# Gates and branch projections with tokens stationary instead of weights

## The chip, the core and the metric

The kernel runs on one core of a Trainium2 chip. Its engines run side by side, each through a queue of its own: PE (TensorE, the matmuls; PEld are its weight loads), DVE (VectorE), ACT (ScalarE), POOL (GpSimd), and SP, which here only issues DMAs. The metric is device microseconds of one execution, the median of several. Before the change it is 1636.45 us (three runs, 1636.2 to 1637.2).

## What is computed

Two layers of an encoder on 256 tokens of 1024 channels, all in f32. A layer has a mixer, a cross-attention into 256 memory tokens, and a SwiGLU feed-forward part. The change is in the mixer:

```python
h = rmsnorm(x)
q, k, v, z, xbc, dt, f_in, gate_logit = split(h @ w_in)
y_attn    = attention(q, k, v) @ w_b_attn             # inner width 512
y_ssd     = gated_norm(ssd(xbc, dt), z) @ w_b_ssd     # inner width 2048
y_fourier = re_fft2(f_in) @ w_b_fourier               # inner width 1536
gates     = sigmoid(gate_logit + gate_bias)           # (256, 3, 1024)
merged    = gates[:, 0] * y_attn + gates[:, 1] * y_ssd + gates[:, 2] * y_fourier
x         = x + merged @ w_out
```

## The kernel before

**Numbers.** Each f32 matrix is split in two parts of the type that the array takes at full speed, hi (rounded) and lo (the rest). A product is three matmuls: hi*hi, hi*lo, lo*hi.

**The weight stream.** All weights lie in HBM in the order of use, in pieces of up to [128, 2048] f32 (1 MB). `load_next` (L312) issues a piece's DMA on SP, `split_next` makes hi with ACT (L322) and lo with DVE (L323); three raw and three split pieces are held. ORDER gives the mixer's order: Fourier columns, B/C, k0, x0, gate 2 (G2), Fourier branch (BF), the columns of q, k, v, x and z mixed, gate 0 (G0) before z0, z2, z3, then the attention branch (BA), gate 1 (G1), and last the SSD branch.

**Two loops of matmuls.** `lin` (L352 to L354) keeps 128 tokens stationary and moves 512 weight columns; the result is rows of tokens. It goes through a piece for the first half of the tokens and then for the second, so two of the four accumulation banks (acc) fill at a time. `lina` (L413 to L415) keeps a [128, 128] block of weights stationary and moves the 256 tokens; the result has the channels on the partitions, which is the layout (F) that the next product needs. Before the change gates and branches are done with `lina`: ACT's tanh takes gate logits out of PSUM with the bias as a per-partition operand (L1013), DVE multiplies the branch's result with 1 + tanh and adds it to the merged sum (L1028 to L1031), and behind the SSD branch ACT and DVE make hi and lo of the sum (L1113, L1114).

**Background tasks.** Convolution, SSD, attention, Fourier and norms are Python generators in four lanes. When the program is built, `pump` is called twice a piece and puts out steps of them for a credit in microseconds; a step that is about to put TensorE's work on fresh results first skips some calls (LATER, SOON), and a step that needs SBUF slots waits until enough are free. `drain_until` and `drain` put out what is left by force: before BF, before BA (all of attention: logits L602, transposes of the softmax L637, values L647, transposes of the joined output L667, hi and lo of it L487 and L488), and before the SSD branch everything (SSD matmuls L847 and L848, results L850 to L852, product with silu(z) L869, squares L870, power L445, scaling L876, transposes L885, hi and lo L487 and L488). Then the framework orders each engine's instructions; an engine runs its own in that order.

Of the kernel before, what the change touches and what calls it, by code (L numbers as in the profile page):

```python
# [43 lines left out]
# ---------------------------------------------------------------- weight stream  # L44
# A piece is [128, nk * n]: nk k-tiles x n columns, at most 2048.
# [3 lines left out]
def stream_plan():  # L49
# [17 lines left out]
    def blocks(w, kt, n):  # L67
        for n0 in range(0, 1024, n):
            plan.append((w, 0, kt, n0, n))

    for tok in ORDER:
# [3 lines left out]
        elif k == "G":  # L75
            for c in range(4):
                wide("w_in", G0 + 1024 * g + 256 * c)
        elif tok == "BF":
            blocks("w_branch_fourier", 12, 128)
        elif tok == "BA":  # L80
            blocks("w_branch_attn", 4, 512)
# [10 lines left out]
    blocks("w_branch_ssd", 16, 128)  # L92
# [20 lines left out]
POFF = [sum(PSIZE[:i]) for i in range(NPIECE + 1)]  # L113


def pack_weights(inputs):
    out = np.empty((L, POFF[-1]), np.float32)
    for l in range(L):
        for i, (w, k0, nk, n0, n) in enumerate(PLAN):
            a = np.asarray(inputs[w])[l, k0 * P:(k0 + nk) * P, n0:n0 + n]  # L120
            out[l, POFF[i]:POFF[i + 1]].reshape(P, nk, n)[...] = a.reshape(nk, P, n).transpose(1, 0, 2)
    return out


# ---------------------------------------------------------------- constants of the shapes
# [8 lines left out]
def shape_consts():  # L134
# [6 lines left out]
    # distances between tokens of the halves by parity: rows for the offsets -1, 0, 1  # L141
    # entry i + j of a row belongs to query i and key 127 - j
# [26 lines left out]
# ---------------------------------------------------------------- kernel  # L169
@with_exitstack  # L170
def trunk(ctx: ExitStack, tc: tile.TileContext, a, out):
# [16 lines left out]
    # Slots of 4 KB and 2 KB for all that comes and goes; a slot's tiles follow in the order of emission.  # L188
# [43 lines left out]
    # ---- background tasks, fed between weight pieces: lanes of generators, each lane in its own order.  # L232
    # A task yields the vector time of what it put out, or LATER or SOON before work of TensorE on what is still under way,
    # or the numbers of 4 KB and 2 KB slots that it is about to take.
# [10 lines left out]
    def step(only=None, force=True):  # L245
        """One step of a background task; False if there is none to run."""
# [48 lines left out]
    # ---- weight stream  # L295
# [4 lines left out]
    def parts(i, n):  # L300
        """The first pieces come by k-tiles, so that the products can start early."""
# [45 lines left out]
    def ordered():  # L347
        """Several accumulations in one bank: TensorE keeps their order."""
        return tc.manual_schedule(engines={mybir.EngineType.PE})
# [6 lines left out]
    # activations in F layout: lists of (hi, lo) tiles [128, 4, 256] per four k-tiles  # L356
    def lin(act, npieces, on_done, nk=8, seg=None, us=BUDGET, par=False, before=None, mid=None):
        """act(kt) -> (hi, lo, index). Pieces come from the stream; on_done(tt, chunk, psum)."""
# [37 lines left out]
    def lina(act, npieces, on_done, us=BUDGET):  # L396
        """Weights stationary: [columns, tokens]. A piece has all k-tiles; on_done(first column, psum [128, nb, 256])."""
# [26 lines left out]
    # ---- constants  # L424
# [12 lines left out]
    def bcast(src, n, tag=None, bufs=2):  # L437
        """A DRAM row of n values on all partitions."""
# [8 lines left out]
    # ---- RMS norm of [128, 1024] rows, then F layout  # L447
    sums = {}

    def square(tt, c):  # L450
        """Sum of the squares of half of X's columns."""
# [25 lines left out]
    def norms(n):  # L477
        """Goes on until no more than n norms are left."""
        drain_until(lambda: len(lanes["n"]) <= n, "n")

    def put_f(pt, hl, tt, scale=None, n=4, par=False):
        """psum [128, n*128] -> hi/lo of an F tile, token half tt."""
# [14 lines left out]
    # ======================================================================= start  # L497
# [40 lines left out]
    # ======================================================================= attention  # L538
    def attn_group(l, g, qt, kt_, vt, gqk, R):
        """qt, kt_, vt: [128, 2, 512] T layout. R: the groups joined so far."""  # L540
# [870 lines left out]
```

## Time and profile before

| | |
|---|---|
| median of the runs | 1636.45 us |
| span of the profiled execution | 1634.2 us |
| TensorE busy | 1618.7 us, 99% |
| VectorE busy | 1155.0 us, 71% |
| ScalarE busy | 972.1 us, 59% |
| GpSimd busy | 46.1 us, 3% |
| read from HBM | 294.44 MB, 181 GB/s |

Of the profiled execution only the span is told, from its first instruction to its last; its whole time is not, and the median stands 2.2 us over that span. A matmul's "us" is its way through a pipe that several share, so the distance of two starts tells what one costs. A wait is named by what ended it.

### The profile page before, as it was taken

The page shows a single profiled execution, that of the slowest core. Times are in us where ns is not written, and L with a number is a line of the kernel's source. Part 1 is how long each engine was busy: PE and PEld are TensorE (multiplying, and loading weights), DVE is VectorE, ACT ScalarE, POOL GpSimd, SP SyncE. Part 2 cuts the span into 40 slices and gives each one's busy share as a digit, 9 for nine tenths or more (in the row PEclk, how much of TensorE's full clock was granted, in tenths as well). Part 3 has the DMA queues.
Part 4 walks back from the last instruction along what each step waited for, and adds up shares of the span by engine and source line. Part 5 has one row for each costly group of instructions (what it writes and reads, how often), then busy time and mean ns, then how long its engine had stood idle before and what let it go on. Part 6 is the DMA issues. An engine that isn't in the chain of part 4 may idle for free.

```text
span 1634.2 us, 25737 instructions
## 1 busy us (share of the span) xinstructions
PE 1618.7 (99%) x10426; PEld 1464.2 (90%) x10426; DVE 1155.0 (71%) x1795; ACT 972.1 (59%) x1661; POOL 46.1 (3%) x47
## 2 busy tenths in 40 slices
PE   7999999999999999999999999999999999999998
PEld 6999988898998888999889999888989988889997
DVE  5898878787967665555477988778888676665543
ACT  6566667777745665444355667677786457554441
POOL 0000000000100100000000000000001001000000
PEclk9999999999999999999999999999999999999999
DMA  8445764545556544655553466645455555445552
GB/s 292 138 156 195 234 205 149 200 166 186 183 180 229 182 155 155 224 182 181 180 187 119 161 206 217 209 161 183 173 181 198 178 208 175 146 158 181 183 189 92
DMA packets 84878, 297.31 MB, mean 182 GB/s; under 512 B 7593, under 2 KB 46889, under 8 KB 54552
## 3 DMA queue, kind: packets, MB, share of 16 engines
q1 hardware_dynamic: 84760, 295.68, 52.9%
q8 instruction: 81, 1.33, 0.3%
q14 instruction: 37, 0.30, 0.1%
HBM read 294.44 MB, written 1.22 MB: 181 GB/s over the span
## 4 chain that ended last, share of the span: by engine, by line
PE 96%; ACT 2%; DVE 1%; DMA 0%; POOL 0%; issue 0%; SPq 0%; DVEq 0%; POOLq 0%
PE acc L354 15%; PE acc L352 15%; PE acc L353 15%; PE acc L414 13%; PE acc L413 13%; PE acc L415 13%; PE tp L847 2%; PE tp L352 1%; PE tp L354 1%; PE tp L353 1%; PE tp L848 1%; PE tp L472 1%; PE tp L647 1%; PE tp L602 1%; ACT wh L322 1%; ACT s L561 1%
## 5 line engine op out<-in xcount | busy, mean ns | idle before, releaser
L323 DVE TENSOR_TENSOR wl<-wr,wh 128x2048 fp32r<-128x2048 f32 (+2 forms) x260 | 573.5, 2208 | 295.3 <-ACT wh L322 294.1
L322 ACT CAST wh<-wr 128x2048 fp32r<-128x2048 f32 (+2 forms) x260 | 477.6, 1840 | 419.3 <-issue 186.5
L413 PE MATMUL acc<-s,wh 128*128 128x256 f32 x1856 | 527.8, 285 | 0.0
L414 PE MATMUL acc<-s,wh 128*128 128x256 f32 x1856 | 526.7, 284 | 0.0
L415 PE MATMUL acc<-s,wl 128*128 128x256 f32 x1856 | 525.6, 283 | 0.0
L352 PE MATMUL acc<-wh,s 128*128 128x512 f32 x1072 | 427.3, 399 | 0.0
L353 PE MATMUL acc<-wl,s 128*128 128x512 f32 x1072 | 423.8, 396 | 0.0
L354 PE MATMUL acc<-wh,s 128*128 128x512 f32 x1072 | 423.4, 395 | 0.0
L413 PEld LDWEIGHTS acc<-s,wh 128*128 128x128 f32 x1856 | 355.9, 192 | 1.6 <-issue 0.9
L414 PEld LDWEIGHTS acc<-s,wh 128*128 128x128 f32 x1856 | 356.1, 192 | 1.3 <-issue 0.5
L415 PEld LDWEIGHTS acc<-s,wl 128*128 128x128 f32 x1856 | 355.9, 192 | 0.0
L354 PEld LDWEIGHTS acc<-wh,s 128*128 128x128 f32 x1072 | 203.5, 190 | 41.5 <-issue 1.4
L352 PEld LDWEIGHTS acc<-wh,s 128*128 128x128 f32 x1072 | 203.8, 190 | 40.8 <-issue 1.9
L353 PEld LDWEIGHTS acc<-wl,s 128*128 128x128 f32 x1072 | 203.6, 190 | 40.5 <-issue 0.9
L688 DVE SCALAR_TENSOR_TENSOR s<-s,cw,s 128x254 f32<-128x254 f32 (+2 forms) x288 | 121.7, 476 | 1.1 <-ACT s L685 0.7
L819 ACT ACTIVATE s<-s,nacs 128x128 f32<-128x128 f32 x128 | 44.6, 393 | 12.3 <-DMA s<-dd 10.6
L352 PE MATMUL tp<-s,s 128*128 128x256 f32 (+1 forms) x176 | 50.3, 287 | 0.0
L354 PE MATMUL tp<-s,s 128*128 128x256 f32 (+1 forms) x176 | 49.9, 285 | 0.0
L353 PE MATMUL tp<-s,s 128*128 128x256 f32 (+1 forms) x176 | 49.7, 283 | 0.0
L822 ACT ACTIVATE s<-s,dt 128x128 f32<-128x128 f32 x128 | 43.9, 395 | 2.7 <-DVE s L603 2.1
L820 DVE SCALAR_TENSOR_TENSOR s<-s,nacs,s 128x128 f32<-128x128 f32 x128 | 41.5, 344 | 3.6 <-ACT s L819 3.6
L823 DVE SCALAR_TENSOR_TENSOR s<-s,dt,s 128x128 f32<-128x128 f32 x128 | 40.1, 344 | 0.0
(216 smaller groups left out, 1417.6 us busy)
## 6 DMA issues: line engine op xcount, KB each, us to landing
wr<-in_wstream SPq DMA_DIRECT2D x236, 1024.0 KB, 4.9
s<-dd SPq DMA_DIRECT2D x32, 512.0 KB, 4.4
wr<-in_wstream SPq DMA_DIRECT2D x16, 768.0 KB, 4.4
s<-vd SPq DMA_DIRECT2D x12, 256.0 KB, 5.7
wr<-in_wstream SPq DMA_DIRECT2D x8, 256.0 KB, 5.1
s<-in_ssd_norm_g SPq DMA_DIRECT2D x8, 256.0 KB, 5.3
s<-in_memT SPq DMA_DIRECT2D x4, 512.0 KB, 5.8
s<-in_c_dft SPq DMA_DIRECT2D x6, 256.0 KB, 5.0
```

Source lines behind the costliest of these rows:

```text
L322: A.copy(hi[:, c], raw[:, c])
L323: V.tensor_sub(lo[:, c], raw[:, c], hi[:, c].bitcast(F32))
L352: T.matmul(o, sh, mh, start=start, stop=False)
L353: T.matmul(o, sh, ml, start=False, stop=False)
L354: T.matmul(o, sl, mh, start=False, stop=stop)
L413: T.matmul(o, hi[:, w0:w0 + P], sh[:, k, :], start=kt == 0, stop=False)
L414: T.matmul(o, hi[:, w0:w0 + P], sl[:, k, :], start=False, stop=False)
L415: T.matmul(o, lo[:, w0:w0 + P], sh[:, k, :], start=False, stop=kt == npk - 1)
L688: V.scalar_tensor_tensor(v[:, b, i0:i1], u[:, b, i0 + k - 3:i1 + k - 3], c[:, k:k + 1], v[:, b, i0:i1], op0=ALU.mult, op1=ALU.add)
L819: A.activation(E[:, j, :], b[:, 1, :], AF.Identity, bias=nacs[:, tt, 32 + hf:33 + hf])
L820: V.scalar_tensor_tensor(E[:, j, :], b[:, 0, :], nacs[:, tt, hf:hf + 1], E[:, j, :], op0=ALU.add, op1=ALU.min)
L822: A.activation(W[:, j, :], cbd[:, tt, 0, :], AF.Copy, scale=dt[:, tt, hf:hf + 1])
```

## The change

Gates and the three branches go through `lin`. Their weights are packed in half pieces of four k-tiles by 512 columns (six pieces of 1 MB for the Fourier branch in place of eight of 768 KB). The bias rows are packed behind the weights; a gate loads its row on all partitions into a 4 KB slot, DVE adds it to the logits, and ACT's tanh follows in place. The merge is done in rows of tokens. Behind the SSD branch each [128, 512] part of the sum becomes a background task: four transposes on TensorE, then hi and lo (`put_f`). Two of the four must be out before the output projection begins, the others after its first piece.

```diff
-    def blocks(w, kt, n):
-        for n0 in range(0, 1024, n):
-            plan.append((w, 0, kt, n0, n))
+    def chunks(w, nh):
+        for n0 in (0, 512):
+            for h in range(nh):
+                half(w, n0, h)
     for tok in ORDER:
         k, g = tok[0], int(tok[1]) if len(tok) > 1 and tok[1].isdigit() else 0
         if k == "f":
             full("w_in", F0 + 512 * g)
         elif k == "G":
-            for c in range(4):
-                wide("w_in", G0 + 1024 * g + 256 * c)
+            full("w_in", G0 + 1024 * g)
+            full("w_in", G0 + 1024 * g + 512)
         elif tok == "BF":
-            blocks("w_branch_fourier", 12, 128)
+            chunks("w_branch_fourier", 3)
         elif tok == "BA":
-            blocks("w_branch_attn", 4, 512)
+            chunks("w_branch_attn", 1)
...
-    blocks("w_branch_ssd", 16, 128)
+    chunks("w_branch_ssd", 4)
...
+NBIAS = 3 * D
...
-    out = np.empty((L, POFF[-1]), np.float32)
+    out = np.empty((L, POFF[-1] + NBIAS), np.float32)
+    out[:, POFF[-1]:] = np.asarray(inputs["gate_bias"])
...
-        gbc = sm([P, 24], "gbc", bufs=1)
-        nc.sync.dma_start(gbc, a["gateb"][l])
-        V.tensor_scalar(gbc, gbc, 0.5, None, op0=ALU.mult)
...
         def gates(b):
-            ga = [s4([P, 4, S]) for _ in range(2)]
-            def f(n0, ps):
-                c = (n0 - G0) // P
-                for j in range(2):
-                    k = c + j - 8 * b
-                    A.activation(ga[k // 4][:, k % 4, :], ps[:, j, :], AF.Tanh, scale=0.5, bias=gbc[:, c + j:c + j + 1])
-            lina(hb, 4, f)
+            ga = [s4([P, D]) for _ in range(2)]
+            o = POFF[-1] + D * b
+            gbb = bcast(a["wstream"][l:l + 1, o:o + D], D)
+            c0 = (G0 + D * b) // 512
+            def f(tt, ch, ps):
+                cs = slice((ch - c0) * 512, (ch - c0) * 512 + 512)
+                g_ = ga[tt][:, cs]
+                V.tensor_add(g_, ps, gbb[:, cs])
+                A.activation(g_, g_, AF.Tanh, scale=0.5)
+            lin(hb, 4, f)
+            free(gbb)
             return ga
         mg = []
-        def branch(act, np_, ga, fin=None):
+        def branch(act, nh, ga, fin=None):
             first = not mg
             if first:
-                mg.extend(s4([P, 4, S]) for _ in range(2))
-            def f(n0, ps):
-                c, n = n0 // P, ps.shape[1]
-                g_, m_ = (t[c // 4][:, c % 4:c % 4 + n, :] for t in (ga, mg))
+                mg.extend(s4([P, D]) for _ in range(2))
+            def f(tt, ch, ps):
+                cs = slice(ch * 512, ch * 512 + 512)
+                g_, m_ = ga[tt][:, cs], mg[tt][:, cs]
                 if first:
                     V.scalar_tensor_tensor(m_, g_, 1.0, ps, op0=ALU.add, op1=ALU.mult)
                 else:
                     V.scalar_tensor_tensor(g_, g_, 1.0, ps, op0=ALU.add, op1=ALU.mult)
                     V.tensor_add(m_, m_, g_)
                 if fin:
-                    fin(c, n, m_)
-            lina(act, np_, f)
+                    fin(tt, ch, m_)
+            lin(act, 2 * nh, f, nk=4 * nh)
...
-                branch(fl(FT), 8, ga)
+                branch(fl(FT), 3, ga)
...
-                branch(fl(R["oT"]), 2, ga)
+                branch(fl(R["oT"]), 1, ga)
...
-        def merge_fin(c, n, m_):
-            hi, lo = (t[:, c % 4:c % 4 + n, :] for t in mT[c // 4])
-            A.activation(hi, m_, AF.Copy, scale=0.5)
-            V.scalar_tensor_tensor(lo, m_, 0.5, hi.bitcast(F32), op0=ALU.mult, op1=ALU.subtract)
-        branch(fl(yT), 8, ga, merge_fin)
-        free(*yT.values(), ga, mg)
+        merged = []
+        def merge_task(tt, ch, m_):
+            yield SOON
+            pt = tp()
+            for k in range(4):
+                T.transpose(pt[:, k * P:(k + 1) * P], m_[:, k * P:(k + 1) * P], idn)
+            put_f(pt, mT[ch], tt, scale=0.5)
+            merged.append((tt, ch))
+            yield 0.6
+        branch(fl(yT), 4, ga, lambda tt, ch, m_: bg(merge_task(tt, ch, m_)))
+        free(*yT.values(), ga)
+        def all_merged():
+            drain_until(lambda: len(merged) == 4, "s")
+            free(mg)
+        drain_until(lambda: len(merged) >= 2, "s")
...
-        lin(fl(mT), 4, residual(gbx, hx), seg=[1, 3])
+        lin(fl(mT), 4, residual(gbx, hx), seg=[1, 3], before=all_merged)
```

Three places in the order of the instructions. Numbers behind a name tell one buffer from another; `wh` and `wl` are parts of weights, `tp` the banks of the background tasks, `idn` the identity of a transpose.

TensorE before, at the last logits matmul (L602) of layer 0, and at the first matmul of its attention branch (L413), 61 wide matmuls later. At the logits:

```order
L354 MATMUL acc1_116<-wh403_4105,s4_9_137 128x512
L352 MATMUL acc1_116<-wh403_4105,s4_8_136 128x512
L353 MATMUL acc1_116<-wl404_4106,s4_8_136 128x512
L602 MATMUL tp1_112<-s4_409_4149,s2_415_4218 128x128
L354 MATMUL acc1_116<-wh403_4105,s4_9_137 128x512
L352 MATMUL acc2_117<-wh403_4105,s4_8_136 128x512
L353 MATMUL acc2_117<-wl404_4106,s4_8_136 128x512
```

At the branch, behind the z columns (acc0) and an SSD matmul (L848):

```order
L353 MATMUL acc0_115<-wl421_4301,s4_8_136 128x512
L354 MATMUL acc0_115<-wh420_4300,s4_9_137 128x512
L352 MATMUL acc0_115<-wh420_4300,s4_8_136 128x512
L353 MATMUL acc0_115<-wl421_4301,s4_8_136 128x512
L848 MATMUL tp1_112<-s2_438_4452,s4_173_1590 128x512
L354 MATMUL acc0_115<-wh420_4300,s4_9_137 128x512
L413 MATMUL acc1_116<-s4_430_4380,wh427_4372 128x256
L414 MATMUL acc1_116<-s4_431_4381,wh427_4372 128x256
```

Attention's later sets (L637, L647, L667) stand among the 61 and are not shown.

TensorE now, at the same logits matmul (L606), 11 wide matmuls before the z columns end:

```order
L358 MATMUL acc3_118<-wh415_3901,s4_9_137 128x512
L356 MATMUL acc0_115<-wh415_3901,s4_8_136 128x512
L606 MATMUL tp1_112<-s4_400_3696,s2_409_3818 128x128
L357 MATMUL acc0_115<-wl416_3902,s4_8_136 128x512
L358 MATMUL acc0_115<-wh415_3901,s4_9_137 128x512
L356 MATMUL acc0_115<-wh415_3901,s4_8_136 128x512
```

and from that end to the branch (L356 on acc1):

```order
L357 MATMUL acc0_115<-wl416_3902,s4_8_136 128x512
L358 MATMUL acc0_115<-wh415_3901,s4_9_137 128x512
L671 MATMUL tp0_111<-idn_121,s4_257_2347 128x128 x4
L641 MATMUL tp2_113<-idn_121,s2_410_3819 128x128 x4
L651 MATMUL tp3_114<-s4_322_2939,s2_411_3820 128x128 x4
L671 MATMUL tp1_112<-idn_121,s4_257_2347 128x128 x4
L852 MATMUL tp3_114<-s2_440_4126,s4_173_1481 128x512
L356 MATMUL acc1_116<-wh418_3933,s4_432_4044 128x512
L357 MATMUL acc1_116<-wl419_3934,s4_432_4044 128x512
```

The softmax's transposes (L641), the values (L651) and the joined output's transposes (L671) of the second half stand in one row between the last z column and the branch, with one SSD matmul (L852); before, they stood among z columns.

VectorE before, in that place, between the softmax's sums (L625) and the joining (L656, L657):

```order
L625 TENSOR_TENSOR rsum272_2695<-rsum272_2695,asc418_4237 128x4
L869 TENSOR_TENSOR s4_331_3275<-s4_331_3275,s4_419_4275 128x512
L626 TENSOR_TENSOR asc418_4237<-asc418_4237 128x4
L627 TENSOR_TENSOR rsum272_2695<-rsum272_2695,asc418_4237 128x4
L629 RECIPROCAL asc418_4237<-rsum272_2695 128x4
L630 TENSOR_TENSOR asc418_4237<-asc418_4237 128x4
L631 TENSOR_TENSOR asc418_4237<-asc418_4237 128x4
L656 TENSOR_SCALAR s4_270_2693<-s4_270_2693,asc418_4237 128x128 x4
L657 SCALAR_TENSOR_TENSOR s4_270_2693<-tp3_114,asc418_4237,s4_270_2693 128x128 x4
```

and now, between the sums (L629) and the joining (L660):

```order
L629 TENSOR_TENSOR rsum259_2349<-rsum259_2349,asc413_3838 128x4
L327 TENSOR_TENSOR wl426_3997<-wr417_3905,wh425_3996 128x2048
L630 TENSOR_TENSOR asc413_3838<-asc413_3838 128x4
L824 SCALAR_TENSOR_TENSOR s4_430_4006<-s4_428_4002,nacs112_941,s4_430_4006 128x128
L631 TENSOR_TENSOR rsum259_2349<-rsum259_2349,asc413_3838 128x4
L824 SCALAR_TENSOR_TENSOR s4_430_4006<-s4_428_4002,nacs112_941,s4_430_4006 128x128
L633 RECIPROCAL asc413_3838<-rsum259_2349 128x4
L824 SCALAR_TENSOR_TENSOR s4_430_4006<-s4_428_4002,nacs112_941,s4_430_4006 128x128
L634 TENSOR_TENSOR asc413_3838<-asc413_3838 128x4
L635 TENSOR_TENSOR asc413_3838<-asc413_3838 128x4
L824 SCALAR_TENSOR_TENSOR s4_430_4006<-s4_428_4002,nacs112_941,s4_430_4006 128x128
L660 TENSOR_SCALAR s4_257_2347<-s4_257_2347,asc413_3838 128x128 x2
```

A weight split (L327) and three steps of the next SSD group (L824) stand between the links of the softmax, where one product of a gate (L869) stood.

TensorE before, at the end of gate 1 and the start of the SSD branch (L413 on acc1):

```order
L414 MATMUL acc0_115<-s4_9_137,wh458_4726 128x256
L415 MATMUL acc0_115<-s4_8_136,wl459_4727 128x256
L885 MATMUL tp0_111<-idn_121,s4_331_3275 128x128 x4
L885 MATMUL tp1_112<-idn_121,s4_331_3275 128x128 x4
L885 MATMUL tp2_113<-idn_121,s4_413_4168 128x128 x4
L885 MATMUL tp3_114<-idn_121,s4_413_4168 128x128 x4
L413 MATMUL acc1_116<-s4_464_4844,wh461_4785 128x256
L414 MATMUL acc1_116<-s4_465_4845,wh461_4785 128x256
```

and now:

```order
L357 MATMUL acc0_115<-wl446_4171,s4_8_136 128x512
L358 MATMUL acc0_115<-wh445_4170,s4_9_137 128x512
L851 MATMUL tp0_111<-s4_360_3316,s4_453_4214 128x64 x8
L852 MATMUL tp1_112<-s2_455_4252,s4_173_1481 128x512
L889 MATMUL tp2_113<-idn_121,s4_202_1780 128x128 x4
L889 MATMUL tp3_114<-idn_121,s4_202_1780 128x128 x4
L889 MATMUL tp0_111<-idn_121,s4_340_3121 128x128 x4
L889 MATMUL tp1_112<-idn_121,s4_340_3121 128x128 x4
L356 MATMUL acc1_116<-wh448_4204,s4_466_4344 128x512
L357 MATMUL acc1_116<-wl449_4205,s4_466_4344 128x512
L356 MATMUL acc2_117<-wh448_4204,s4_466_4344 128x512
L357 MATMUL acc2_117<-wl449_4205,s4_466_4344 128x512
```

In front of the branch stand now the last SSD group's matmuls (L851, L852) too, and the transposes (L889) of the first gated group (`s4_202`), which the branch's first matmul needs; before, these two stood further ahead. The fourth group's transposes, in front of the branch before, stand behind 24 of its matmuls now.

## Rows read from the trace of the kernel before

**Rows 1.** The page's head.

```profile
span 1634.2 us, 25737 instructions
PE 1618.7 (99%) x10426; PEld 1464.2 (90%) x10426; DVE 1155.0 (71%) x1795; ACT 972.1 (59%) x1661; POOL 46.1 (3%) x47
```

**Rows 2.** The page, costliest groups: count, then busy us, mean ns.

```profile
L413 PE MATMUL acc<-s,wh 128*128 128x256 f32 x1856 | 527.8, 285 | 0.0
```

**Rows 3.** PE's timeline in the SSD branch, 57 matmuls: start us, us, what.

```profile
469.72 0.28 PE L413 MATMUL acc<-s,wh 128*128 128x256 f32 x1
...
476.44 0.28 PE L415 MATMUL acc<-s,wl 128*128 128x256 f32 x1
```

**Rows 4.** PE's timeline in the last down projection, 20 matmuls.

```profile
1599.68 0.39 PE L354 MATMUL acc<-wh,s 128*128 128x512 f32 x1
...
1603.99 0.39 PE L352 MATMUL acc<-wh,s 128*128 128x512 f32 x1
```

**Rows 5.** Busy us (instructions) of PE, PEld, DVE, ACT, POOL; PEclk; DMA.

```profile
396.00:406.00 10.00, 10.00 (x60) 8.42 (x58) 8.48 (x38) 9.93 (x29) 0.00 (x0) 1.00 0.78 207
406.00:416.00 10.00, 10.00 (x53) 8.05 (x52) 9.95 (x22) 9.70 (x26) 0.00 (x0) 1.00 0.34 99
...
447.00:457.00 10.00, 10.00 (x88) 10.00 (x87) 5.79 (x6) 6.42 (x9) 0.17 (x1) 1.00 0.69 236
```

**Rows 6.** The chain of waits: start us, us, what.

```profile
406.97 0.86 PE tp L848 x2
...
423.58 0.84 PE tp L847 x8
...
454.26 1.75 PE tp L885 x16
```

**Rows 7.** Groups by line, columns as in rows 2.

```profile
L1013 ACT ACTIVATE s<-acc,gbc 128x256 f32<-128x256 f32 x48 | 20.2, 467 | 0.0
...
L1130 DVE TENSOR_TENSOR X<-X,acc 128x512 f32<-128x512 f32 x24 | 16.4, 683 | 26.1 <-PE acc L354 26.1
```

**Rows 8.** DMA issues: count, KB each, us to landing.

```profile
s<-in_xattn_norm_g SPq DMA_DIRECT2D x2, 512.0 KB, 3.7
```

**Rows 9.** PE's timeline before and at the attention branch.

```profile
395.35 0.39 PE L602 MATMUL tp<-s,s 128*128 128x128 f32 x2
...
416.90 0.28 PE L413 MATMUL acc<-s,wh 128*128 128x256 f32 x1
```

**Rows 10.** ACT's timeline there.

```profile
410.58 1.12 ACT L487 CAST s<-tp 128x512 fp32r<-128x512 f32 x2
```

**Rows 11.** DVE's timeline there.

```profile
397.09 0.34 DVE L603 SCALAR_TENSOR_TENSOR s<-tp,ars,s 128x128 f32<-128x128 f32 x1
...
413.29 1.28 DVE L488 TENSOR_TENSOR s<-tp,s 128x512 fp32r<-128x512 f32 x2
```

**Rows 12.** Groups by line, of the SSD tasks and the weight split.

```profile
L323 DVE TENSOR_TENSOR wl<-wr,wh 128x2048 fp32r<-128x2048 f32 (+2 forms) x260 | 573.5, 2208 | 295.3 <-ACT wh L322 294.1
...
L851 DVE TENSOR_TENSOR s<-tp,el 128x512 f32<-128x512 f32 x16 | 11.0, 686 | 1.2 <-PE tp L848 0.9
...
L870 ACT ACTIVATE s<-s 128x512 f32<-128x512 f32 x16 | 10.1, 632 | 0.2
```

**Rows 13.** The instructions on tile gst: min/median/max ns.

```profile
L876 DVE SCALAR_TENSOR_TENSOR s<-s,gst,s x16: 742/746/754, 336.3 to 1256.7; 128x512 f32<-128x512 f32 x16
...
L445 POOL TENSOR_TENSOR gst<-gst,half_c x8: 695/696/2777, 335.5 to 1255.3; 128x2 f32<-128x2 f32 x8
```

**Rows 14.** PE's timeline, its last matmul.

```profile
1629.60 0.39 PE L354 MATMUL acc<-wh,s 128*128 128x512 f32 x1
```

**Rows 15.** A stretch at the end, columns as in rows 5.

```profile
1633.85:1634.20 0.35, 0.00 (x0) 0.00 (x0) 0.00 (x0) 0.00 (x0) 0.00 (x0) 0.50 0.00 0
```

**Rows 16.** The chain of waits at the start.

```profile
12.08 0.43 PE acc L353
...
16.41 0.23 PE acc L353
```

## The prediction

> **What bounds the kernel now.** I read the page first: the span is 1634.2 us, and TensorE's queue is busy for 1618.7 us of it [rows 1]. Matmuls overlap in the pipe, so that figure is not yet proof; the starts are. In the group view each of the three lines of the weights-stationary loop stands with 1856 matmuls of 256 columns, and the mean of 285 ns is a latency [rows 2]. In the timeline 57 of them follow each other from 469.72 to 476.44: 6.72 us over 56 steps, 120 ns from start to start [rows 3]. In the tokens-stationary loop 20 matmuls of 512 columns go from 1599.68 to 1603.99: 4.31 over 19, 227 ns [rows 4]. 256 columns cost 120 and 512 cost 227, so the columns cost 107 ns per 256, and each matmul brings about 13 ns with it. TensorE is the bound nearly everywhere, at the upper of its two clocks (2.4 GHz; granted 1.00 in the stretches I asked for [rows 5]), so whatever shortens its stream counts in full, and so does whatever makes it wait.
>
> The second thing to see is how near VectorE and ScalarE come to being the bound at the end of the mixer: around the attention branch they are busy 8.5 to 9.95 and 9.7 to 9.9 of 10 us, against 5.8 and 6.4 some 40 us later [rows 5]. The kernel holds there only because the background work comes early enough.
>
> **The change, part by part.** *The matmuls.* In a layer the three gates are 576 matmuls of 256 columns, the Fourier branch 288, attention 96, SSD 384: 1344, and 2688 in two layers, 322.6 us at 120 ns. They become 1344 of 512 columns, 305.1 us at 227 ns: **17.5 us less**, all of it on the path. The stationary tiles are contiguous in tokens, as in the loop of rows 4.
>
> The Trainium skill has another rule for this (TensorE: Matmul & The Clock Gate, section "Wait — 56ns, not 53.3ns?"): a warm matmul starts one column per 2.4 GHz cycle plus about 2.5 ns after the one before. By it the swap would give only 1344 times 2.5 ns, 3.4 us, and the sum below would come out 14 us higher. The rows show 13 ns beside the columns here, so the measurement decides.
>
> *The transposes.* 16 a layer are new, 109 ns each, as 16 take 1.75 us [rows 6]: 32 of them, **3.5 us more**. Their conversion to two parts replaces as much conversion by halves of a bank.
>
> *VectorE and ScalarE.* Each gate gets four adds from PSUM with the bias row, at 683 ns like the residual's add; ScalarE's tanh goes from 48 tiles at 467 ns to 24 of twice the width [rows 7]. VectorE's 12 adds are 8.2 us a layer, and the merges, in operations twice as wide, give a part of it back. This lies beside TensorE; its cover is thin only at the end of the mixer, where it adds to what follows below. The six bias rows are 512 KB each, like the gain row that lands in 3.7 us [rows 8]; they stand on SP's queue between weight loads that run three pieces ahead, so I cost them at nothing, and 3.7 us once if that lead were gone.
>
> *What moves.* The background tasks are fed after each half piece. Six pieces in the Fourier branch instead of eight are four feedings fewer, and each bias row holds a slot that the tasks ask for. In the built order the tasks slide back: the last logits matmul of attention had 61 wide matmuls between it and the attention branch, and has 11 now; the first gate's transposes stand 144 later, and the last SSD group's final set, which stood before and inside the attention branch, stands behind all of the last gate, where the drain puts it out by force.
>
> *First wait: the attention branch.* Its first matmul needs the attention output in both token halves. In the trace that chain (logits, softmax, transposes, values, joining, transposes, rounding) starts at the last logits matmul, over at 395.7, and ends with ScalarE's second rounded half at 411.70 [rows 9, 10]; the branch starts only at 416.90, with 5.2 us to spare, 2.3 us for VectorE's lower half, ready at 414.57 [rows 9, 11]. So 16.0 us. In the new order TensorE has 11 matmuls (2.5 us) for it, the chain's own four sets (12 transposes at 109 ns, 1.3, and four f32 matmuls for the values, 0.8 to 0.9 like the four of an SSD set, which the trace counts as eight) and one SSD matmul of 0.86 [rows 6]: 5.6 us. It waits for the rest, **10.4 us a layer, 20.8 in all**. Behind this matmul stands all the rest of TensorE's stream, and the branch has taken all four banks, so no gate matmul goes ahead of it. Counted from VectorE's read of the logits at 397.09 [rows 11] the chain is 14.6 us, the wait 9.0. The upper end is one more weight split (2.2 us [rows 12]) ahead of a link, 12.7. I take 10.4, the whole chain as measured, since in the new order a weight split stands ahead of that read as well. No wait at all is the first rival. The lower halves add nothing: eight matmuls and the SSD set lie between.
>
> *Second wait: the SSD branch.* Its first matmuls need the first gated group, whose transposes now come after the last gate. From the gate's last matmul on TensorE has the set of eight SSD matmuls (twice 0.84), one of 0.86, 16 transposes (1.75) and four wide matmuls (0.91): 5.3 us [rows 6]. VectorE reads the set's result when that is over (1.7), the other one at 2.7, each 0.69, and is through at 3.3; then come a split (2.2), an add (0.69) and the lower half (0.64), with the delays between engines 7.0 us [rows 11, 12]. It waits 1.7 us. The fourth group's transposes come 20 matmuls (4.5 us) later; for them VectorE has three more halves, a product, ScalarE's square (0.63, and its sum), GpSimd's power (0.70) and a scaling (0.75) [rows 12, 13]: another 1.0. **2.7 us a layer, 5.4 in all.** It can be nothing, if the lower half is ready with the upper one, and 6 with one more split and a second wait of that size.
>
> *The end of the branch.* The last two merged tiles are transposed behind the first piece of the output projection (5.45 us); VectorE needs two passes of 0.7 us by then and the lower halves are wanted 21 matmuls later. I cost this at nothing; behind three splits it would be a microsecond.
>
> **The sum.** 1634.2 − 17.5 + 3.5 + 20.8 + 5.4 = 1646.4 us of span. The runs' median of 1636.45 lies 2.2 us over the profiled span: **1648.6 us**.
>
> **The rivals.** *Hidden (1622.4).* The tasks are later in the order but not late on the engines; only 17.5 and 3.5 count: 1620.2 and 2.2. For it: the order is a scheduler's, and TensorE hardly waits today. Against it: the scheduler found nothing to put between the four dependent sets, and the two queues they pass through were full. It decides if the chain takes under 5.6 us.
>
> *Half the chain (1632.6).* A TensorE that waits feeds the queues less, so the 16 us shrink to 8 and the wait to 2.4: 16 us less than forecast.
>
> *The clock falls (1654.6).* After the last matmul, started at 1629.60, TensorE is idle and the granted clock stands at 0.50 at 1633.85 [rows 14, 15]. At the start wide matmuls come 0.43 us apart at 12.08 and 0.23 at 16.41 [rows 16]. If the first wait does this, some 4 us of matmuls run at 1.2 GHz, 2 us lost, and the chain's own sets take a microsecond longer: 3 us, twice. The Trainium skill says that an idle stretch gates the clock to half until sustained work releases it (TensorE: Matmul & The Clock Gate, section "HAM oscillation — how this bites in real kernels"); no matmul of this trace after a wait shows it. I leave it out of the forecast because the sets inside the wait break it up.
>
> *Two engines full (1659.8).* VectorE's added adds keep it behind: 12.7 and 6 us.
>
> **How the numbers follow.** Forecast 0.50, clock 0.20, half the chain 0.12, hidden 0.10, full engines 0.08. A measurement of this kernel tells about 0.2% (3.3 us) from no change. Faster: hidden and a third of half the chain, 0.14. Same: the rest of that and the forecast's lower edge, 0.12. Slower: 0.74. The range 1632 to 1658 leaves out the hidden case and the full engines; the forecast's own is 1643 to 1654.
>
> **What would show it.** Matmuls of the moved lines 227 ns apart, and 120 nowhere in gates and branches; TensorE idle some 10 us ahead of the first attention-branch matmul, released by ScalarE's rounding or VectorE's joining, and under 3 us at the SSD branch; PEclk at 1.00 or 0.50 behind that. Were TensorE dense there, the second and larger half of this sum would be wrong.

## The result, and the profile after

The changed kernel takes 1658.74 us (median of 4 runs, 1656.85 to 1659.51), the kernel before 1636.83: a ratio of 1.013 (95%: 1.0118 to 1.0142), 21.9 us more. Forecast were 1648.6 us, 12.2 more. The direction is right, the size is not.

The head of the page after, to be read against [rows 1]:

```profile
span 1657.7 us, 23062 instructions
PE 1619.8 (98%) x9114; PEld 1401.0 (85%) x9114; DVE 1163.1 (70%) x1781; ACT 961.6 (58%) x1621; POOL 43.0 (3%) x47
...
PEclk9999999999899999999999999999989999999999
```

PE has 1312 matmuls fewer and is still busy for 98% of a longer span: a wait of a few us, twice, does not show in that figure. The row PEclk shows two slices that are not at 9. The cadence came as forecast. In the SSD branch 96 wide matmuls start between these two (columns as in [rows 3]), 95 steps in 21.68 us, 228 ns [rows 4]:

```profile
474.28 0.49 PE L356 MATMUL acc<-wh,s 128*128 128x512 f32 x1
...
495.96 0.39 PE L358 MATMUL acc<-wh,s 128*128 128x512 f32 x1
```

The gates' new adds and the wider tanh, group view (columns as in [rows 7]), are where they were priced, 0.68 us an add:

```profile
L1015 DVE TENSOR_TENSOR s<-acc,s 128x512 f32<-128x512 f32 x24 | 16.4, 684 | 0.3 <-PE acc L358 0.3
L1016 ACT ACTIVATE s<-s 128x512 f32<-128x512 f32 x24 | 15.1, 628 | 32.9 <-DVE s L1015 32.9
```

What PE waited for in the mixer's last stages of layer one, by line (us in total, times, longest us). The same view of the kernel before has no row over the same places. L671, L641 and L651 are the attention chain's sets, L594 transposes of queries in the z stage, L358 the SSD branch:

```profile
PE tp L671 <- DVE s L661: 2.8, 2, 2.6
PE tp L641 <- ACT s L619: 2.1, 1, 2.1
PE tp L651 <- ACT s L642: 2.0, 1, 2.0
PE tp L594 <- DVE s L492: 1.9, 1, 1.9
PE acc L358 <- DVE s L492: 1.5, 1, 1.5
```

PE's timeline through the first of these waits (start us, us, what, idle before and who ended it), to be read against [rows 9]:

```profile
408.61 0.38 PE L606 MATMUL tp<-s,s 128*128 128x128 f32 x2
...
411.15 0.39 PE L358 MATMUL acc<-wh,s 128*128 128x512 f32 x1
411.38 0.60 PE L671 MATMUL tp<-idn,s 128*128 128x128 f32 x4
414.04 1.63 PE L641 MATMUL tp<-idn,s 128*128 128x128 f32 x4 [2.06 <-ACT s L619]
417.65 2.07 PE L651 MATMUL tp<-s,s 128*128 128x128 f32 x8 [1.98 <-ACT s L642]
422.33 0.73 PE L671 MATMUL tp<-idn,s 128*128 128x128 f32 x2 [2.60 <-DVE s L661]
...
423.76 1.92 PE L852 MATMUL tp<-s,s 128*128 128x512 f32 x2
424.68 1.42 PE L356 MATMUL acc<-wh,s 128*128 128x512 f32 x1
425.90 0.63 PE L357 MATMUL acc<-wl,s 128*128 128x512 f32 x1
...
428.42 0.40 PE L357 MATMUL acc<-wl,s 128*128 128x512 f32 x1
428.65 1.89 PE L851 MATMUL tp<-s,s 128*128 128x64 f32 x16
```

The last logits matmuls (L606) start at 408.61, the branch at 424.68. Between them stand the 11 wide matmuls and the four sets that the prediction counted. In layer two the pattern is the same (1228.09 and 1244.14). The wide matmuls behind the wait come 0.43 us apart until 428.4, then 0.23. The stretch of the lower clock in each layer (columns as in [rows 5]; the third figure from the right is PEclk):

```profile
414.70:428.35 13.65, 8.84 (x24) 5.88 (x24) 11.20 (x32) 7.81 (x20) 0.00 (x0) 0.50 0.28 98
1233.90:1247.55 13.65, 8.89 (x24) 5.79 (x25) 11.47 (x32) 8.08 (x21) 0.00 (x0) 0.50 0.29 107
```

The granted clock is 0.50 in these two stretches, and 1.00 in the rest from 18.75 us to the end of the matmuls: 0.50 is the lower of the two levels, 1.2 GHz.

A table from the same timelines tells where the time went. At equal work done (the first wide matmul of a stage, with the same number of columns gone through ahead of it), it gives the start in the kernel after against the kernel before, and the same for the variant `a_calls` of the next section, in us:

| reached | after | a_calls |
|---|---|---|
| first gate in the stream (G2), layer one | +2.0 | +1.1 |
| v0 (G2 and Fourier branch done) | -3.7 | -2.0 |
| last matmul of the z columns | -5.1 | -3.3 |
| attention branch (BA) | +7.8 | -3.3 |
| SSD branch | +9.9 | -4.4 |
| output projection | +11.4 | -5.3 |
| layer two starts | +12.7 | -3.9 |
| last matmul of the z columns, layer two | +5.6 | -8.3 |
| attention branch | +18.5 | -8.3 |
| SSD branch | +20.4 | -10.0 |
| output projection | +21.9 | -10.9 |
| feed-forward part | +23.6 | -9.7 |

The stages with the new loop gain; between the last z column and the first matmul of the attention branch 12.9 us are lost in each layer, 2 more up to the SSD branch, and 1.5 in that branch. A part of this is the matmuls of tasks that stand there now and stood elsewhere before.

### The profile page after: what moved, and what is told of

Its sections match the earlier page's. It is cut to its first block, busy times and chain, and to the rows that moved or that the text cites. A ratio compares the mean times of both kernels' runs of the same rounds, so it can differ in the third digit from the quotient of the medians.

```text
span 1657.7 us, 23062 instructions
## 1 busy us (share of the span) xinstructions
PE 1619.8 (98%) x9114; PEld 1401.0 (85%) x9114; DVE 1163.1 (70%) x1781; ACT 961.6 (58%) x1621; POOL 43.0 (3%) x47
## 4 chain that ended last, share of the span: by engine, by line
PE 90%; DVE 5%; ACT 2%; issue 1%; POOL 1%; DMA 1%; SPq 0%; DVEq 0%; ACTq 0%; POOLq 0%
PE acc L356 19%; PE acc L357 19%; PE acc L358 19%; PE acc L417 7%; PE acc L418 7%; PE acc L419 7%; DVE wl L327 2%; PE tp L851 2%; PE tp L356 1%; PE tp L358 1%; PE tp L357 1%; PE tp L852 1%; PE tp L651 1%; PE tp L606 1%; DVE s L692 1%
## 5 line engine op out<-in xcount | busy, mean ns | idle before, releaser
L327 DVE TENSOR_TENSOR wl<-wr,wh 128x2048 fp32r<-128x2048 f32 (+1 forms) x256 | 572.8, 2240 | 305.3 <-ACT wh L326 303.7
L326 ACT CAST wh<-wr 128x2048 fp32r<-128x2048 f32 (+1 forms) x256 | 477.1, 1867 | 382.6 <-PE acc L358 185.8
L356 PE MATMUL acc<-wh,s 128*128 128x512 f32 x1520 | 608.0, 400 | 0.0
L357 PE MATMUL acc<-wl,s 128*128 128x512 f32 x1520 | 599.2, 394 | 0.0
L358 PE MATMUL acc<-wh,s 128*128 128x512 f32 x1520 | 595.4, 393 | 3.0 <-DVE s L492 3.0
L358 PEld LDWEIGHTS acc<-wh,s 128*128 128x128 f32 x1520 | 287.7, 189 | 62.5 <-DVE s L492 3.9
L356 PEld LDWEIGHTS acc<-wh,s 128*128 128x128 f32 x1520 | 289.2, 190 | 60.2 <-ACT s L491 1.6
L417 PE MATMUL acc<-s,wh 128*128 128x256 f32 x960 | 273.2, 285 | 0.0
L419 PE MATMUL acc<-s,wl 128*128 128x256 f32 x960 | 272.4, 284 | 0.0
L418 PE MATMUL acc<-s,wh 128*128 128x256 f32 x960 | 272.1, 283 | 0.0
L417 PEld LDWEIGHTS acc<-s,wh 128*128 128x128 f32 x960 | 184.0, 192 | 0.6 <-issue 0.4
L418 PEld LDWEIGHTS acc<-s,wh 128*128 128x128 f32 x960 | 184.0, 192 | 0.4
L419 PEld LDWEIGHTS acc<-s,wl 128*128 128x128 f32 x960 | 184.0, 192 | 0.0
L692 DVE SCALAR_TENSOR_TENSOR s<-s,cw,s 128x255 f32<-128x255 f32 (+2 forms) x288 | 122.1, 476 | 0.5
L358 PE MATMUL tp<-s,s 128*128 128x256 f32 (+1 forms) x176 | 50.0, 285 | 0.0
L356 PE MATMUL tp<-s,s 128*128 128x256 f32 (+1 forms) x176 | 49.8, 285 | 0.0
L492 DVE TENSOR_TENSOR s<-tp,s 128x512 fp32r<-128x512 f32 x56 | 36.6, 684 | 5.5 <-ACT s L491 5.4
```

The lines of the kernel that those rows point to most:

```text
L326: A.copy(hi[:, c], raw[:, c])
L327: V.tensor_sub(lo[:, c], raw[:, c], hi[:, c].bitcast(F32))
L356: T.matmul(o, sh, mh, start=start, stop=False)
L357: T.matmul(o, sh, ml, start=False, stop=False)
L358: T.matmul(o, sl, mh, start=False, stop=stop)
L417: T.matmul(o, hi[:, w0:w0 + P], sh[:, k, :], start=kt == 0, stop=False)
```

## The experiments

**Four calls.** The plan for the Fourier branch went from eight pieces to six, so its 16 feedings of the background tasks (`pump`) became 12 of the same amount in all. A step that yields LATER or SOON is passed over for four or three *calls*, whatever credit they bring. In `a_calls` the Fourier branch alone gets its 16 calls back:

```
+        us = us * 0.75 if more else us
...
                     if tt == 1:
                         done(i, us)
                     else:
                         pump(us / 2)
+                    if more:
+                        calls[0] += 1
+                        if calls[0] % 3 == 0:
+                            pump(us / 2)
```

`done` calls `pump` too, so these are the 12 calls, and every third brings one more.

> The changed kernel, with four more feedings of the background tasks in the Fourier branch (16 calls of three quarters of the amount, in place of 12), so that as many calls are made there as in the kernel before. Theory 1 (the waits come from the missing calls alone): the last logits matmul has its 61 wide matmuls ahead of the attention branch again, no wait of TensorE there, at the SSD branch or ahead of the attention transposes in the third z stage is over 0.7 us, the granted clock stays at 1.00 to the end, and the time is 1636.8 - 17.5 + 3.5, 1623 us, or 1625 if the later start of the changed kernel's profile (1.5 to 2 us) belongs to the change. Rival (the loop itself: VectorE's 24 added adds and the bias rows keep the tasks late on the engines): the order is as in the kernel before, but TensorE still waits several us at the attention branch, and the time is 1640 or more.

1626.41 us, ratio 0.9938 (0.9926 to 0.9951): 32 us faster than the changed kernel and 10 faster than the one before, 1 to 3 us over what theory 1 gave. Its page, its one wait of PE from 384 to 476 us, and the clock in the stretch that was slow in the changed kernel:

```profile
span 1624.6 us, 23060 instructions
PE 1607.0 (99%) x9114; PEld 1395.1 (86%) x9114; DVE 1162.7 (72%) x1781; ACT 964.8 (59%) x1625; POOL 44.7 (3%) x47
```

```profile
PE tp L895 <- DVE s L886: 0.3, 1, 0.3
```

```profile
414.70:428.35 13.65, 13.54 (x67) 10.95 (x67) 12.63 (x19) 11.96 (x15) 0.00 (x0) 1.00 0.39 134
```

The wait that is left is 0.3 us at a gated group's transposes, and the clock stays at 1.00 to the end of the matmuls. So the tokens-stationary loop was not what cost the time. `b_fewer_calls` does the reverse, in the kernel before: `lina` leaves out every fourth call in the Fourier branch and makes the others larger by a third.

> The kernel before, with four feedings fewer in the Fourier branch (12 calls of four thirds of the amount, in place of 16) and nothing else. Theory 1: the weights-stationary kernel gets the same waits without any of the change: the last logits matmuls stand right ahead of the attention branch, a wait of 10 to 14 us a layer there with the granted clock at 0.50 in it and behind it, 2 us or more in each of the two other places, 1660 to 1675 us. Rival (the loop itself): the weights-stationary kernel has room on VectorE and swallows the later order, 1637 to 1642 us.

1683.24 us, 1.0286 (1.0268 to 1.0305): 46.6 us slower, more than I had expected. PE's waits in layer one, and the clock at the branch:

```profile
PE tp L639 <- ACT s L617: 5.0, 1, 5.0
PE tp L775 <- ACT s L579: 3.5, 1, 3.5
...
```

```profile
423.20:430.00 6.80, 4.98 (x17) 3.55 (x18) 5.37 (x23) 3.56 (x15) 0.70 (x1) 0.50 0.28 111
```

The logits themselves stand right ahead of the branch there (L604, 416.77 and 417.70), and more of the chain is bare: 5.0 us for ScalarE's softmax in one piece, and 3.5 ahead of transposes (L775) in the z stage.

**The bias rows.** `a_no_bias_row`: `gbb = X[:, 0, :]` in place of the row loaded into a slot. It leaves out the bias (a row of X is added instead, so the gates' values are others) and keeps the adds.

> The changed kernel, with the gates' bias rows not loaded and no slot taken for them (rows of X, which lie in SBUF, are added in their place, so the gates' values are others). Theory 1: the order is the same and so are the waits, 1657 to 1659 us. Rival (the bias rows' transfers or the slot that they hold make the tasks late): the waits shrink, 1640 to 1652 us. If the later start of the changed kernel's profile came from the bias rows, the first matmul starts 1.5 us earlier here.

1658.8 us, 1.0132 (1.0119 to 1.0146), the changed kernel's time. Neither their transfers nor the slot matter. Its first wide matmul starts at 13.24 us, no earlier.

**Two calls, many calls.** As `a_calls`, with 14 and with 24 calls.

> The changed kernel with two more feedings in the Fourier branch in place of four (14 calls, the same amount in all). In the built order the last logits matmul has 61 wide matmuls ahead of the attention branch, as with four; with one more feeding it has 11, as in the changed kernel. Theory 1 (a call more or less decides whether a task finds its slots or misses a round, so the loss comes in one piece): the whole loss is gone, 1626 to 1629 us. Rival (every missing call costs its share): half of the 32 us are left, 1640 to 1645 us.

> The changed kernel with 24 feedings in the Fourier branch (the same amount in all). Theory 1: more calls than the 16 of the kernel before buy nothing, since no wait is left for them to remove: 1625.5 to 1627 us. Rival (calls are short in the changed kernel elsewhere too, and the 3 to 4 us that it lacks to the forecast come from that): 1623 to 1625 us.

24 calls: 1626.67 us, 0.9938 (0.9923 to 0.9952), the same as 16. 14 calls: 1636.99 us, 1.0001 (0.9992 to 1.001), which neither theory said. With one more call the built order has the changed kernel's 11 wide matmuls behind the last logits, with two it has 61; that part does come in one piece. But the chain's last transposes stand 9 to 14 matmuls ahead of the branch, 28 to 30 with four calls. What PE waits for then:

```profile
PE acc L357 <- DVE wl L327: 1.4, 1, 1.4
PE tp L857 <- DVE s L840: 1.3, 1, 1.3
```

```profile
418.00:424.00 6.00, 3.31 (x18) 2.34 (x17) 6.00 (x13) 5.91 (x9) 0.00 (x0) 1.00 0.00 0
424.00:430.00 6.00, 6.00 (x25) 5.09 (x24) 6.00 (x7) 4.27 (x8) 0.00 (x0) 0.72 0.92 314
```

It waits for VectorE: once for a product of the SSD task, once for the low half of a weight split, with VectorE busy in 6.00 of 6.00 us, and the clock falls again (0.72). This looks like the rival "two engines full", in a kernel where the first wait is gone; no run took work off VectorE there to show it.

**The clock.** To see what its fall costs beside the wait, matmuls that nobody reads were put between the chain's sets. `a_filled_wait` puts eight behind each step of the chain (48 a layer in its trace, where the expectation says 47), `a_filled_wait_2` eight ahead of each of the first five (40, where it says 41). The second one's loop:

```
+  spare = acc()
+  for nf in (8, 8, 8, 8, 8):
+      ...
+      for _ in range(nf):
+          T.matmul(spare, h[0][0][:, 0, 0:P], h[0][0][:, 0:2, :] ..., start=True, stop=True)
+      if not step("a"):
+          step()
   drain_until(lambda: "oT" in R and R.get("a"), "a")
```

> The changed kernel, with 47 matmuls of 512 columns a layer put between the sets of the attention chain; their operands lie ready, and nobody reads what they write. TensorE is then busy in the wait, and the chain itself is as before. Theory (the clock fell because TensorE waited, and that is a cost of its own): granted clock 1.00 throughout, the wide matmuls behind the wait 227 ns apart, which gives back 2.1 us a layer, and the chain's own sets at full speed, up to 2.6 us a layer more: 1649 to 1655 us. Rival (the lower clock is hidden in the wait, which the chain on the other engines sets): 1657 to 1661 us, whatever the clock does.

1658.08 us, 1.0131 (1.0117 to 1.0145): no gain that can be told, and inside the rival's range, although the clock stayed at 1.00 through the chain in both layers. But seven filling matmuls stood behind the last set, where ScalarE had been done for 0.8 us, the SSD sets had moved, and in layer two the clock fell at another wait (0.50 from 1206.39 to 1209.80 us); so it decides nothing.

> The changed kernel with 41 matmuls of 512 columns a layer between the sets of the attention chain (16, 11, 6 and 8), none behind the last set, so that nothing but the chain stands ahead of the attention branch and the order of all else is the changed kernel's. In the first filling some 0.8 us of it ran on after the chain was done and the SSD sets had moved. Theory (the fall of the clock is a cost beside the wait): granted clock 1.00 throughout, the eight wide matmuls behind the wait in 1.8 us and not 4.0, the chain done no later: 1652 to 1655 us. Rival (hidden: what TensorE gains there it waits for later, or the chain on the other engines sets it): 1657 to 1660 us.

1654.63 us, 1.0109 (1.0094 to 1.0124): 4.1 us less than the changed kernel, with 40 more matmuls in each layer. The first set of L671 stands behind the values (L651) here, not ahead of the softmax's transposes. PE's timeline:

```profile
410.00 0.39 PE L358 MATMUL acc<-wh,s 128*128 128x512 f32 x1
...
421.32 0.60 PE L671 MATMUL tp<-idn,s 128*128 128x128 f32 x4
421.75 1.02 PE L852 MATMUL tp<-s,s 128*128 128x512 f32 x2
422.65 0.50 PE L356 MATMUL acc<-wh,s 128*128 128x512 f32 x1
422.98 0.39 PE L357 MATMUL acc<-wl,s 128*128 128x512 f32 x1
...
424.37 0.39 PE L357 MATMUL acc<-wl,s 128*128 128x512 f32 x1
424.60 1.89 PE L851 MATMUL tp<-s,s 128*128 128x64 f32 x16
```

From the last wide matmul to the branch it is 12.65 us (410.00 to 422.65), 13.53 in the changed kernel (411.15 to 424.68): 0.9 us for the sets at the upper level. The eight wide matmuls take 1.95 us to the next set, 3.97 before: 2.0 us. So 2.9 us a layer belong to the clock (2.8 in layer two by the same starts), and the wait itself stays. Of the 5.8 in all 1.6 were lost again, in layer two, where the clock fell at another wait (L594), at which it had stayed at 1.00 in the changed kernel:

```profile
418.00:424.00 6.00, 6.00 (x30) 4.43 (x29) 6.00 (x26) 4.60 (x12) 0.00 (x0) 1.00 0.51 175
424.00:430.00 6.00, 6.00 (x36) 5.24 (x35) 5.00 (x12) 2.46 (x8) 0.00 (x0) 1.00 0.00 0
1203.00:1206.00 3.00, 2.65 (x15) 2.33 (x16) 1.84 (x4) 1.73 (x5) 0.00 (x0) 0.82 1.03 329
1206.00:1209.00 3.00, 3.00 (x12) 2.54 (x12) 1.64 (x3) 1.13 (x4) 0.00 (x0) 0.61 0.40 164
```

**The start.** The profile of the changed kernel starts its first wide matmul 1.5 us later than the one before (11.28). `b_longer_rows` is the kernel before with the weights' rows as long as in the changed one: `np.zeros((L, POFF[-1] + 3 * D))`.

> The kernel before, with the packed weights' rows longer by 3072 zeros a layer, as in the changed kernel; nothing loads them. Theory (the later start of the changed kernel's profiles, 0.9 to 2.0 us, comes from where its weights lie): the first wide matmul starts 1 to 2 us later than at 11.3 us, and the time is 1637.5 to 1638.5 us. Rival (it comes from the start of the profiled execution, or from other instructions): starts at 11.0 to 11.6 us, 1636 to 1637.2 us.

1637.12 us, 1.0002 (0.9992 to 1.0011). The first wide matmul of the changed kernel, and of this one:

```profile
12.74 0.79 PE L356 MATMUL acc<-wh,s 128*128 128x512 f32 x1
```

```profile
12.22 0.79 PE L352 MATMUL acc<-wh,s 128*128 128x512 f32 x1
```

0.9 us of the later start is there without the rest of the change, and too small for the time to show. But programs that are alike up to there differ among themselves, some later and some earlier than the kernel before (13.24 us without bias rows, 11.76 with 14 calls, 10.62 in `a_calls_no_bias` below), with one profile each, so what makes the start stays open.

**More room for the tasks.** Three orders of the stream on top of `a_calls`, with the first gate moved towards the attention branch: `z1 x3 z0 G0 z2 z3 BA G1` and so on.

> The changed kernel with the four calls given back, and the first gate one place later in the stream (behind z0; before it stood ahead of z0). In the built order the last logits matmul has 92 wide matmuls ahead of the attention branch (61 without the move) and the first gated group's transposes stand 24 behind its start (108 without). Theory 1 (what the kernel with the calls still lacks to 1622 us are the 0.7 to 1.4 us that the gated groups' transposes and the SSD sets wait in the last gate and the SSD branch of each layer): earlier tasks take that away, 1623.5 to 1625.5 us. Rival (VectorE is full there, and an earlier task only moves the wait): 1626 to 1628 us.

> As the one before, with the first gate behind z2: 77 wide matmuls behind the last logits matmul, the gated groups' transposes 120 behind the branch's start. Theory 1: the attention chain has more room, which was not wanted, and the transposes stand where they stood: 1626 to 1627 us. Rival: 1623.5 to 1625.5 us.

> As the ones before, with the first gate right ahead of the attention branch: 62 wide matmuls behind the last logits matmul, the first two gated groups' transposes 22 ahead of the branch. Theory 1: as with the first move, 1623.5 to 1625.5 us. Rival (VectorE full): 1626 to 1628 us.

1630.10 us (0.9963, 0.9949 to 0.9977), 1631.19 (0.9969, 0.9957 to 0.9981) and 1631.37 (0.9968, 0.9956 to 0.9979): all three are slower than `a_calls`, and both theories missed. In the first, PE waits in the z stage for attention's VectorE work, and the clock falls behind it:

```profile
PE tp L586 <- DVE s L578: 2.6, 1, 2.6
```

```profile
378.00:384.00 6.00, 6.00 (x28) 4.90 (x28) 4.54 (x14) 4.01 (x5) 0.00 (x0) 0.76 0.59 200
```

**The added adds.** `a_calls_no_bias` is `a_calls` with `A.activation(g_, ps, AF.Tanh, scale=0.5)` straight from PSUM. It leaves out the gates' bias and the adds with it, so the gates' values are others.

> The changed kernel with the four calls given back, and without the gates' bias: no bias rows, no adds on VectorE; ScalarE takes the tanh of the logits straight from PSUM (the gates' values are others). That takes 24 adds at 684 ns, 16.4 us, off VectorE. Theory (the 3 to 4 us that the kernel with the calls lacks to the sum without waits are VectorE's added adds in the last gate and the SSD branch): 1622.5 to 1624.5 us, and the 0.7 us a layer of added waits in each of these two stages are gone. Rival (TensorE is the bound and VectorE's adds lie beside it): 1625.5 to 1627 us.

1625.16 us, 0.9929 (0.9915 to 0.9942), 1.2 us less than `a_calls` (the two intervals overlap), and between the ranges of the two theories. From the last gate's end through the SSD branch PE's steps beyond their usual length fall from 1.0 us a layer to 0.2. But a single wait of 1.1 us for ScalarE in layer one's output projection, and smaller ones, took that back: from the first wide matmul to the last it is 1607.9 us here (10.62 to 1618.51) and 1607.7 in `a_calls` (12.21 to 1619.94). What the profile gains is its earlier start, whose cause is open. So it is not shown that the adds cost `a_calls` anything in all.

## Why the prediction was wrong, point by point

**The loops** (-17.5) **and the transposes** (+3.5) hold. In `a_calls`, where no wait covers them, the usual steps of all PE's instructions sum to 1579.9 us against 1595.1: 15.2 less, where I had 14.0. By the 2.5 ns beside the columns that the Trainium skill gives (TensorE: Matmul & The Clock Gate, section "Wait — 56ns, not 53.3ns?") the loops would have given only 3.4, an estimate; the rows decide for 13 ns.

**The first wait** was right as a size: 10.4 a layer forecast. From the next wide matmul after the last logits (408.75) to the branch it is 15.9 us (I had 16.0), less the 5.6 that I counted as cover, 10.3. That it fits so closely is partly luck: 0.9 of it is the lower clock in the sets, so at the upper clock it would be 9.4. PE's waits there sum to only 6.9 us in the view above; the sets took longer than I had counted (1.63 us for L641 and 2.07 for L651, counted at 0.44 and 0.84). The links are not quite those of before: ScalarE loads a table and makes a whole weight part between two links, and VectorE's low half of that part (2.29 us) stands ahead of the next. ScalarE's rows first, then VectorE's:

```profile
412.20 1.28 ACT L619 ACT_TABLE_LOAD   x1
...
415.15 1.88 ACT L326 CAST wh<-wr 128x2048 fp32r<-128x2048 f32 x1
417.04 0.56 ACT L642 COPY s<-tp 128x512 f32<-128x512 f32 x1
...
424.00 0.62 ACT L491 CAST s<-tp 128x512 fp32r<-128x512 f32 x1 [0.78 <-PE tp L671]
```

```profile
411.01 0.68 DVE L617 TENSOR_REDUCE asc<-s 128x4 f32<-128x512 f32 x1
...
417.06 2.29 DVE L327 TENSOR_TENSOR wl<-wr,wh 128x2048 fp32r<-128x2048 f32 x1 [1.07 <-ACT wh L326]
```

So neither "hidden" nor "half the chain" came true: a TensorE that waits left the two queues ahead of the links no shorter here.

**The step that failed** is the sentence that left the clock out "because the sets inside the wait break it up". They don't: the clock fell in the middle of the sets, at 414.70 and in layer two at 1233.90, and stayed down behind the branch's start. The rival had priced it at 3 us a layer, two behind the wait and one in the sets; `a_filled_wait_2` shows 2.0 and 0.9. Since the measured chain has the sets' 0.9 in it already, the sum lacks 2.0 a layer, 4 us. The Trainium skill (TensorE: Matmul & The Clock Gate, section "HAM oscillation — how this bites in real kernels") tells of waits between dense bursts of matmuls, behind which TensorE starts again at half its clock. The rows agree with it here, with waits of 2.0 to 2.6 us and small sets between them, but not at the lone wait of 1.9 us (L594), where 1.00 stayed; I had set it aside.

**A wait that I had not listed** is the second part. The tasks slide back, and I priced what that does at the two branches alone. The transposes of the group that is gated first (L889 at 379.86 and 381.17) stand among the z columns now; their place 144 matmuls later was in my text, but I gave it no price. The query transposes (L594) behind them wait 1.9 us until VectorE has read such a bank (L492), which comes behind a weight split (L327). With smaller ones PE's steps there are 2.0 us a layer longer than before: 4 us. PE's row, then VectorE's:

```profile
387.64 0.66 PE L594 MATMUL tp<-idn,s 128*128 128x128 f32 x4 [1.90 <-DVE s L492]
```

```profile
384.71 2.28 DVE L327 TENSOR_TENSOR wl<-wr,wh 128x2048 fp32r<-128x2048 f32 x1
```

**The second wait** was oversized a little: 1.5 us at L358 as the view has it (1.7 and 1.0 forecast for its two parts), 2.1 us a layer with all small ones in the SSD branch, for 2.7. **The end of the branch**, costed at nothing, costs 0.4 a layer more than the transposes.

The sum again, for the profiled execution: 12.2 - 1.2 (loops and transposes) + 4.0 (clock) + 4.0 (the wait not listed) - 1.1 (second) + 0.8 (end) + 2.0 (start, up to the first gate) = 20.7 of 23.5 us of span; 2.8 are spread over steps that I did not assign. Of the start 1.5 are the later first wide matmul, which may not belong to the change.

**Why the tasks were late** I had put down to two things, four feedings fewer and the slots of the bias rows. The first is shown alone to be enough (`a_calls`, `b_fewer_calls`), the second to be nothing. That the slide was a side effect of the plan, and could be had without, I had not asked; it decides the sign of the change. Why two calls tip the last logits and one does not I read only from the built order.

## What to carry to other kernels

Where background work is fed by the piece, a new tiling of the stream changes how often it is fed: count the calls before and after, and keep them. Price every place that a later task touches, not the largest one. A wait of TensorE costs its length, and where the clock falls in it the lower clock besides, 2.9 us a layer at the attention branch here.

The version that beats both is `a_calls`: 1626.4 us, 0.62% under the kernel before.

## What was not expected of the hardware

Four sets of transposes and small matmuls, spread over the 13.5 us between the last z column and the branch, did not keep the clock up: it was at 0.50 for 13.65 us in either layer, 6 us of them behind the last long wait. At a single wait of 1.9 us (L594) it stayed at 1.00 in the changed kernel in both layers, and fell in layer two of `a_filled_wait_2` (0.61 in the stretch behind it).
